# A Mamba-2 mixer in an fp32 decoder trunk: another order of its first projections, other owners of its buffers

## The chip, the cores and the metric

The kernel runs on one core of a Trainium2 chip. The metric is device time in microseconds for one launch, the median of three runs. The engines: PE (TensorE, matmuls), DVE (VectorE), ACT (ScalarE), POOL (GpSimd) and SP (SyncE, which here only issues DMAs). Lnnn is a line of the kernel before; behind the first changed line the kernel after has other numbers, by up to 16.

## What is computed

A decoder trunk of two layers on 256 tokens with D = 2048, in float32: an attention mixer (MLA), an MLP, a Mamba-2 mixer (SSM), an MLP, each with RMSNorm ahead and a residual around it. The change lies in the Mamba-2 mixer:

```python
def ssm_mixer(h, w_in, conv_w, conv_b, dt_bias, a_log, d_skip, norm_g, w_out):
    zxbcdt = h @ w_in                                   # 2048 x (4096 z + 4096 x + 1024 B + 1024 C + 64 dt)
    z, xbc, dt = jnp.split(zxbcdt, ...)
    xbc = silu(causal_depthwise_conv(xbc, conv_w, conv_b))      # width 4
    xs, b_in, c_in = jnp.split(xbc, ...)                        # 8 groups of 8 heads of 64
    dt = softplus(dt + dt_bias);  a = -exp(a_log)
    y = ssd_chunked_scan(xs, dt, a, b_in, c_in)                 # one chunk of 256 tokens here
    y = (y + d_skip * xs) * silu(z)
    y = group_rms_norm(y) * norm_g
    return y @ w_out
# the scan of one chunk, per group g and head h
    cum = cumsum(dt * a);  decay = exp(cum_l - cum_s) for s <= l
    y = ((c @ b.T) * decay) @ (x * dt)
```

## The kernel before

**Weights.** The products run in fp32r pieces: a weight tile of 128 x 1024 (a *unit*) comes in by DMA (`wraw`, six buffers), ACT rounds it to `wh` (L102), DVE forms the rest `wl = wraw - wh` (L103), and PE multiplies high and low parts (L339, L340, L343). A plain unit is 12 matmuls of 128x128 by 128x512. Units are taken in one fixed sequence through the whole kernel, and wraw520, wh520 and wl520 are those of unit 520. `wh` and `wl` have four buffers each, so ACT and DVE run up to four units ahead of PE.

**Seven-product pairs.** The first four x blocks of the input projection are done as two pairs, each by a scheme with seven products (M1, N7, N5, N6, N4, M2, N3) of four units where eight would stand. Such a unit is 6 matmuls (L1158 to L1160) and is used with sums of tokens (`sN5` and so on) and sums of weights, which DVE forms (L183) beside its own wl: 40 DVE operations for 28 units. N7's result holds one of the two `sm` banks of PSUM for the whole pair. Between the products stand plain units of other x blocks, the fillers; `woven` interleaves them by a model of PE's and DVE's time.

**Order.** PE's order is written by hand: the program text is its order. Small work is put among the units by `later(n, fn)`: fn runs n ticks on, and a tick is two plain units. The other engines' order comes from a scheduler that goes by dependencies and priorities; `behind(...)` ties an instruction behind the latest weight load or half.

**The mixer.** B and C come in two blocks each; `conv` transposes a block half into a PSUM bank (L1216), and the convolution along the free axis is one ACT operation (L1222) and three DVE operations (L1225) per 128 channels, out of that bank. The narrow dt block ends in a fold into an sm bank (L367) and a chain of small DVE and ACT operations. The x blocks are written to DRAM (`xD`) and read back shifted: `x_conv(g)` loads the group's tile `xtm`, its shifted copies `tap` and the taps' weights `cw` on SP's queue, DVE combines them (L1353, L1354). Per group `cb_group` forms c·bᵀ in an sm bank; `pump`, once each tick, takes a head's row of `cum` from DRAM, broadcast to 128 partitions (`cm`, issued on ACT's queue, L1407), and `head` turns it into the decay `mt` on ACT (L1417, L1419). `products` multiplies a group's heads (L1437) into both `yp` banks of PSUM, POOL adds the skip (L1441, with the gain `dsk`) and the far part (L1443). `z_block` gates; `words` has POOL copy parts of the result by DMA (`tr`, L308), PE transposes it into an sm bank (L322), ACT and DVE split it (L299, L300), and the so units multiply it. Gains (`dsk`, `sng`, 256 KB each) are loaded on SP's queue into two `gb` buffers (L391). `SSM_ORDER` is the order of the blocks: v is an x convolution (v1+2: two ticks late), z a gate block, o an output block.

## Time and profile before

| | before |
|---|---|
| median of three runs (lowest to highest) | 2331.21 us (2329.78 to 2332.99) |
| the profiled execution: its time; its span | 2331.0 us; 2329.2 us |
| PE, DVE, ACT, POOL busy, of the span | 2281.0, 1971.9, 1437.2, 254.7 us |
| mean granted clock of PE | 0.992 |
| DMA | 569.74 MB, mean 245 GB/s |

The span is the profiled execution from its first to its last instruction; 1.8 us of its time lie around it, and its time is 0.2 us under the median. A busy time is a sum over one engine; a matmul that waits on the pipeline counts as busy. In a row of the timeline stand the start, the length, the engine, the line, the output and inputs and, in brackets, how long the engine had been idle and what ended that. A window's row has the share of full speed that PE's clock was granted.

### The profile page before, as it was taken

Reading aid. Unit: us, or ns where it says so; the run is one execution under the profiler, and the core shown is the slowest. Engines: PE = TensorE matmul, PEld = TensorE weight load, DVE = VectorE, ACT = ScalarE, POOL = GpSimd, SP = SyncE. Lnnn points to the kernel's source line nnn. Section 1 sums busy time; section 2 is a strip of 40 time slices with the busy share of each in tenths; the row PEclk is TensorE's granted clock in tenths of the full one; section 3 lists DMA queues with packets and bytes.
Section 4 is the critical chain, followed back from the end, with each engine's and each line's share of the span. In section 5 each row is a group of like instructions: output and inputs, shape, how many; then the busy total and the mean of one; then the engine's idle time right before and its main releaser. Section 6 shows DMA issues by size and latency. Waiting matters only on the chain.

```text
span 2329.2 us, 30832 instructions
## 1 busy us (share of the span) xinstructions
PE 2281.0 (98%) x10881; PEld 1886.9 (81%) x10881; DVE 1971.9 (85%) x2257; ACT 1437.2 (62%) x2036; POOL 254.7 (11%) x323
## 2 busy tenths in 40 slices
PE   9999999999999999989998899999999999999999
PEld 7888888888888888877876677788888888888887
DVE  7786798899899888898768888876989899989985
ACT  7775566666666656556656665564666666666663
POOL 1540000000000000000001322230000000000000
PEclk9999999999999999999999999999999999999999
DMA  8545688888888877768886887777688888888875
GB/s 316 166 160 163 210 244 254 262 254 262 277 246 261 279 211 251 245 176 268 290 310 220 297 269 252 265 222 216 214 257 244 267 266 252 261 269 243 267 233 164
DMA packets 177050, 569.74 MB, mean 245 GB/s; under 512 B 20192, under 2 KB 29344, under 8 KB 176896
## 3 DMA queue, kind: packets, MB, share of 16 engines
q1 hardware_dynamic: 150112, 502.44, 64.6%
q0 software_dynamic: 15040, 52.68, 11.0%
q10 hardware_dynamic: 11744, 12.66, 1.8%
q8 instruction: 85, 1.39, 0.2%
q14 instruction: 69, 0.57, 0.1%
HBM read 542.23 MB, written 6.41 MB: 236 GB/s over the span
## 4 chain that ended last, share of the span: by engine, by line
PE 88%; DVE 5%; DMA 4%; ACT 2%; issue 1%; POOL 0%; SPq 0%; ACTq 0%; DVEq 0%
PE yp L619 9%; PE yp L618 9%; PE yp L617 9%; PE acc L339 8%; PE acc L343 8%; PE acc L340 8%; PE st L618 7%; PE st L619 7%; PE st L617 7%; DMA cm<-cumD 2%; DVE wl L103 2%; PE st L1160 1%; PE st L1158 1%; PE st L1159 1%; PE yp L339 1%
## 5 line engine op out<-in xcount | busy, mean ns | idle before, releaser
L102 ACT ACTIVATE wh<-wraw 128x1024 fp32r<-128x1024 f32 (+1 forms) x818 | 856.1, 1052 | 522.4 <-PE acc L340 183.9
L103 DVE TENSOR_TENSOR wl<-wraw,wh 128x1024 fp32r<-128x1024 f32 (+1 forms) x818 | 999.3, 1240 | 197.9 <-ACT wh L102 186.4
L617 PE MATMUL yp<-wh,k 128*128 128x512 f32 x896 | 349.3, 390 | 0.0
L619 PE MATMUL yp<-wh,k 128*128 128x512 f32 x896 | 348.8, 389 | 0.0
L618 PE MATMUL yp<-wl,k 128*128 128x512 f32 x896 | 348.6, 389 | 0.0
L102 ACT ACTIVATE wh<-wrx 128x1024 fp32r<-128x1024 f32 x192 | 203.3, 1059 | 169.8 <-PE yp L619 102.9
L103 DVE TENSOR_TENSOR wl<-wrx,wh 128x1024 fp32r<-128x1024 f32 x192 | 233.7, 1222 | 40.7 <-ACT wh L102 40.2
L339 PE MATMUL acc<-wh,k 128*128 128x512 f32 x496 | 197.6, 398 | 3.0 <-ACT wh L102 3.0
L619 PEld LDWEIGHTS yp<-wh,k 128*128 128x128 f32 x896 | 168.2, 188 | 35.1
L618 PEld LDWEIGHTS yp<-wl,k 128*128 128x128 f32 x896 | 168.2, 188 | 34.9
L617 PEld LDWEIGHTS yp<-wh,k 128*128 128x128 f32 x896 | 168.2, 188 | 34.8
L339 PE MATMUL acc<-wh,xt 128*128 128x512 f32 x480 | 193.0, 402 | 2.7 <-ACT wh L102 1.7
L340 PE MATMUL acc<-wh,k 128*128 128x512 f32 x496 | 193.8, 391 | 0.0
L340 PE MATMUL acc<-wh,xt 128*128 128x512 f32 x480 | 188.9, 394 | 0.0
L617 PE MATMUL st<-wh,xt 128*128 128x512 f32 x448 | 177.7, 397 | 0.0
L619 PE MATMUL st<-wh,xt 128*128 128x512 f32 x448 | 174.9, 390 | 0.0
L618 PE MATMUL st<-wl,xt 128*128 128x512 f32 x448 | 174.7, 390 | 0.0
L343 PE MATMUL acc<-wl,k 128*128 128x512 f32 x496 | 133.8, 392 | 4.5 <-DVE wl L103 4.5
L617 PE MATMUL st<-wh,sN 128*128 128x512 f32 x336 | 133.1, 396 | 0.0
L618 PE MATMUL st<-wl,sN 128*128 128x512 f32 x336 | 131.5, 391 | 0.9 <-DVE wl L103 0.8
L619 PE MATMUL st<-wh,sN 128*128 128x512 f32 x336 | 131.1, 390 | 0.0
L343 PE MATMUL acc<-wl,xt 128*128 128x512 f32 x480 | 129.4, 392 | 0.1
(343 smaller groups left out, 3700.2 us busy)
## 6 DMA issues: line engine op xcount, KB each, us to landing
wraw<-mi SPq DMA_DIRECT2D x256, 512.0 KB, 5.6
wraw<-mo SPq DMA_DIRECT2D x256, 512.0 KB, 5.4
wraw<-si SPq DMA_DIRECT2D x160, 512.0 KB, 5.3
wraw<-so SPq DMA_DIRECT2D x64, 512.0 KB, 4.7
wrx<-mi SPq DMA_DIRECT2D x56, 512.0 KB, 5.1
wrx<-mi POOLq DMA_DIRECT2D x56, 512.0 KB, 7.7
wraw<-wo SPq DMA_DIRECT2D x32, 512.0 KB, 3.9
tap<-xD SPq DMA_DIRECT2D x24, 512.0 KB, 7.4
```

The source lines that it names most:

```text
L102: self.last = nc.scalar.activation(h[:, v], raw[:, v], AF.Copy)
L103: self.last_lo = nc.vector.tensor_tensor(lo[:, v], raw[:, v], h[:, v].bitcast(F32), ALU.subtract)
L339: nc.tensor.matmul(accs[t][:, :n], ah, wh[:, q, :], start=first and kt + q == 0, stop=False)
L340: nc.tensor.matmul(accs[t][:, :n], al, wh[:, q, :], start=False, stop=False)
L343: nc.tensor.matmul(accs[t][:, :n], lhs(kt + q, t)[0], wl[:, q, :], start=False, stop=en and q == nk - 1)
L617: nc.tensor.matmul(b, ah, wh, start=first and q == 0, stop=False)
L618: nc.tensor.matmul(b, ah, wl, start=False, stop=False)
L619: nc.tensor.matmul(b, al, wh, start=False, stop=last and q == 1)
L1158: nc.tensor.matmul(bank[onto], ah, wh, start=done + q == 0 and not skip, stop=False, skip_group_check=skip)
L1159: nc.tensor.matmul(bank[onto], al, wh, start=False, stop=False, skip_group_check=skip)
L1160: nc.tensor.matmul(bank[onto], ah, wl, start=False, stop=done == 3 and q == 1, skip_group_check=skip)
```

## The change

It does seven things, all in the mixer; PE has the same matmuls in another order.

1. Order of the first blocks: B0, dt, C0 and x4 come as plain blocks before the pairs (B0, C0, dt before). The sums of tokens are made in ticks 5, 8 and 11 (0, 1 and 2 before). The fold of dt comes 2 ticks after its block (6 before).
2. Fillers: both pairs have 12 plain units (8 and 16 before): x5 and half of x6, then the rest of x6 and x7.
3. Shared buffers: the pools `xn` (sums N7 and N6, then `xtm`) and `rx` (weights of the pairs, then `tap`) live on through the mixer, so that the first convolution, `x_conv(0, 0)`, is called inside the second pair, once N5 and N6 are complete.
4. A convolution half of B and C is copied out of its PSUM bank by ACT (`held`), and always uses an sm bank (`wide=False`).
5. `pump` keeps four `cm` in flight and takes a head when more than two are there.
6. The gains of the groups are loaded on POOL's queue.
7. `SSM_ORDER`, the steps inside `x_conv` and the depth of `cb` (2 buffers in place of 5) follow.

On PE the first place is the fold of dt. Before, it stands in the first pair, behind C0's second half; `sm_755` is the half's bank, `sm_758` the fold's, `st` a product's sum, and 455 and 456 are units:

```order
L1216 MATMUL sm_755_9552<-ident_97,s2_741_9227 128x128
L1216 MATMUL sm_755_9552<-ident_97,s2_742_9229 128x128
L367 MATMUL sm_758_9569<-cst_96,s2_744_9270 128x64 x2
L1158 MATMUL st_750_9369<-wh456_9509,sN6_724_8955 128x512
L1159 MATMUL st_750_9369<-wh456_9509,sN6_725_8956 128x512
L1160 MATMUL st_750_9369<-wl456_9510,sN6_724_8955 128x512
```

After, it stands between two plain units, those of C0 (`acc`), ahead of the pairs:

```order
L343 MATMUL acc_722_9058<-wl433_9063,xt_677_8587 128x512
L343 MATMUL acc_723_9059<-wl433_9063,xt_677_8587 128x512
L367 MATMUL sm_733_9165<-cst_96,s2_721_9056 128x64 x2
L339 MATMUL acc_722_9058<-wh434_9080,xt_690_8693 128x512
L340 MATMUL acc_722_9058<-wh434_9080,xt_691_8694 128x512
```

No convolution half stands around it any more, and no product holds a bank.

On ACT the second place is a group's heads. Before (group 1), the loads of heads 12 and 13 and their use:

```order
L1407 DMA cm12_11368<-cumD_8833 128x256
L1407 DMA cm13_11370<-cumD_8833 128x256
L102 ACTIVATE wh549_11316<-wraw549_11173 128x1024
L1222 ACTIVATE s2_814_11285<-sm_813_11280,cst_96 128x256
L1417 ACTIVATE mt12_11437<-cm12_11368,pcum_8830 128x128 x2
L1419 ACTIVATE mt12_11437<-mt12_11437,lndt_8832 128x128 x2
L1417 ACTIVATE mt12_11437<-cm13_11370,pcum_8830 128x128
L102 ACTIVATE wh550_11334<-wraw550_11244 128x1024
```

After, the loads in that place are those of heads 14 and 15, and heads 12 and 13, which are used there, were loaded earlier:

```order
L1417 DMA cm14_11437<-cumD_8833 128x256
L102 ACTIVATE wh551_11374<-wraw551_11261 128x1024
L1232 ACTIVATE s2_821_11297<-s2_819_11286 128x512
L1417 DMA cm15_11439<-cumD_8833 128x256
L1427 ACTIVATE mt12_11515<-cm12_11368,pcum_8830 128x128 x2
L1429 ACTIVATE mt12_11515<-mt12_11515,lndt_8832 128x128
L102 ACTIVATE wh552_11392<-wraw552_11314 128x1024
```

Between load and use stood one unit's wh; now heads 14 and 15 are loaded before head 12 is taken.

On SP the third place is the first convolution's loads. Before, they stand at plain units, behind wraw525 and wraw527:

```order
L85 DMA wraw525_10552<-si 128x1024
L1348 DMA xtm0_10531<-xD_8834 128x2x512
L1336 DMA cw0_3_10571<-cwx 128x512
L1340 DMA tap0_2_10573<-xD_8834 128x2x512
L1336 DMA cw0_2_10575<-cwx 128x512
L1340 DMA tap0_1_10577<-xD_8834 128x2x512
L85 DMA wraw526_10579<-si 128x1024
L85 DMA wraw527_10597<-si 128x1024
L1336 DMA cw0_1_10615<-cwx 128x512
L1340 DMA tap0_0_10617<-xD_8834 128x2x512
```

After, they stand behind wraw520 and wraw522, which are products of the second pair:

```order
L85 DMA wraw520_10519<-si 128x1024
L1353 DMA xtm0_10539<-xD_8834 128x2x512
L1340 DMA cw0_3_10541<-cwx 128x512
L1344 DMA tap0_2_10543<-xD_8834 128x2x512
L1340 DMA cw0_2_10545<-cwx 128x512
L1344 DMA tap0_1_10547<-xD_8834 128x2x512
L85 DMA wraw521_10549<-si 128x1024
L85 DMA wraw522_10573<-si 128x1024
L1340 DMA cw0_1_10595<-cwx 128x512
L1344 DMA tap0_0_10597<-xD_8834 128x2x512
```

The loads moved forward by five units; xtm0 and tap0 now lie in the shared pools. In DVE's order after, the product `tap0_1` with `cw0_1` stands ahead of wl520.

Besides: group 7's two transposes stood ahead of unit 648 on PE and now stand ahead of unit 658, which reads them; in POOL's order each gain load stands directly behind the instruction that reads its buffer last, or that instruction's transposed words.

The diff, without the lines that only follow from these:

```diff
-    def gain_tile(self, src):
+    def gain_tile(self, src, queue=None):
         t = self.gb.tile([P, 512], F32, tag="gb", name=self.name("gb"))
-        self.nc.sync.dma_start(t, src)
+        (queue or self.nc.sync).dma_start(t, src)
...
         def put(name, src):
-            S[name] = [pool.tile([P, 8, P], F32R, name=self.name("s" + name)) for _ in range(2)]
+            if name in ("N7", "N6"):
+                S[name] = [xn.tile([P, 8, P], F32R, tag="xn", name=self.name("s" + name)) for _ in range(2)]
+            else:
+                S[name] = [pool.tile([P, 8, P], F32R, name=self.name("s" + name)) for _ in range(2)]
             self.split_out(*[v.rearrange("p k n -> p (k n)") for v in S[name]], src)
...
             if done == 3:
                 after(name)
+                if name in ("N5", "N6") and count.get("N5") == count.get("N6") == 4 and free:
+                    free()
             self.spend(1.36)
...
-                a = self.scratch()
+                a, held = self.scratch(), self.scratch()
+                nc.scalar.activation(held, b, AF.Copy)
...
-                    s, o = b[:, k * 256:(k + 1) * 256], a[:, k * 256:(k + 1) * 256]
+                    s, o = held[:, k * 256:(k + 1) * 256], a[:, k * 256:(k + 1) * 256]
...
-        def bc_block(name, i, lag=1, gap=2, wide=True):
+        def bc_block(name, i, lag=1, gap=2, wide=False):
...
         def dt_block():
-            self.narrow_block(("si", "dt", 0, 0), self.xT, dt_chain, 6)
+            self.narrow_block(("si", "dt", 0, 0), self.xT, dt_chain, 2)
...
-            pairs = [sp1.tile([P, S], F32, tag="dts", name=f"dt{i}", bufs=3).rearrange("p (i t h) -> p i t h", i=2, t=2) for i in range(3)]
+            pairs = [sp.tile([P, 512], F32, tag="cw", name=f"dt{i}", bufs=3)[:, :S].rearrange("p (i t h) -> p i t h", i=2, t=2)
+                     for i in range(3)]
...
-            self.later(4, cums)
+            self.later(3, cums)
...
-            t = sp2.tile([P, 384], F32, tag="cb", name=f"cb{g}", bufs=5)
+            t = sp2[0].tile([P, 384], F32, tag="cb", name=f"cb{g}", bufs=2)
...
         def x_conv(g, wait):
-            xt = sp2.tile([P, 2, 512], F32, tag="xtm", name=f"xtm{g}", bufs=4)
-            x = [xt[:, t] for t in range(2)]
-            cw, tap = {}, {}
+            cw, tap, xts = {}, {}, []
 
             def weight(k):
-                cw[k] = sp2.tile([P, 512], F32, tag="cw", name=f"cw{g}_{k}", bufs=3)
+                cw[k] = sp.tile([P, 512], F32, tag="cw", name=f"cw{g}_{k}", bufs=3)
                 nc.sync.dma_start(cw[k], d["cwx"][g][:, k * 512:(k + 1) * 512])
 
             def load(k):
-                tap[k] = sp2.tile([P, 2, 512], F32, tag="tap", name=f"tap{g}_{k}", bufs=3)
+                tap[k] = self.flow.pools["rx"].tile([P, 2, 512], F32, tag="rx", name=f"tap{g}_{k}")
                 nc.sync.dma_start(tap[k], x_rows(g, 0, 2, k))
...
             def whole():
-                nc.sync.dma_start(xt, x_rows(g, 0, 2))
+                xts.append(xn.tile([P, 2, 512], F32, tag="xn", name=f"xtm{g}"))
+                nc.sync.dma_start(xts[0], x_rows(g, 0, 2))
...
             def total():
-                tapped(0)
-                nc.vector.tensor_tensor(xt, xt, both(4), ALU.add)
-                tap[3] = sp2.tile([P, 2, 512], F32, tag="tap", name=f"th{g}", bufs=3)
+                with behind("last_lo"):
+                    plus(both(4))
+                    tapped(0)
+
+            def tanh():
+                tap[3] = self.flow.pools["rx"].tile([P, 2, 512], F32, tag="rx", name=f"th{g}")
                 with behind("last"):
-                    nc.scalar.activation(tap[3], xt, AF.Tanh, scale=0.5)
+                    nc.scalar.activation(tap[3], xts[0], AF.Tanh, scale=0.5)
 
             def silu():
-                nc.vector.scalar_tensor_tensor(xt, tap[3], 1.0, xt, ALU.add, ALU.mult)
+                with behind("last_lo"):
+                    nc.vector.scalar_tensor_tensor(xts[0], tap[3], 1.0, xts[0], ALU.add, ALU.mult)
 
             def ahead():
-                xg[g] = x
-                for i in range(8):
-                    hq.append((g, i))
+                x = xg[g] = [xts[0][:, t] for t in range(2)]
...
             self.later(wait, lambda: fetch(whole, lambda: weight(3), lambda: load(2), lambda: weight(2), lambda: load(1)))
             self.later(wait + 1, lambda: fetch(lambda: weight(1), lambda: load(0)))
-            self.later(wait + 2, lambda: cb_group(g))
             self.later(wait + 3, mult)
             self.later(wait + 4, lambda: tapped(1))
-            self.later(wait + 5, total)
-            self.later(wait + 6, lambda: (silu(), ahead()))
+            self.later(wait + 4, lambda: cb_group(g))
+            self.later(wait + 5, lambda: (total(), hq.extend((g, i) for i in range(8))))
+            self.later(wait + 6, tanh)
+            self.later(wait + 7, lambda: (silu(), ahead()))
 
         def pump():
             for _ in range(2):
-                if cms:
+                if len(cms) > 2 or cms and not hq:
                     g, i, cm = cms.pop(0)
                     head(g, i, cm)
                     if i == 7:
                         break
-            while hq and len(cms) < 2:
-                g, i = hq.pop(0)
-                cm = sp2.tile([P, S], F32, tag="cm", name=f"cm{8 * g + i}", bufs=4)
-                nc.scalar.dma_start(cm, cumD[8 * g + i:8 * g + i + 1].to_broadcast([P, S]))
-                cms.append((g, i, cm))
+            for _ in range(2):
+                if hq and len(cms) < 4:
+                    g, i = hq.pop(0)
+                    cm = sp2[0].tile([P, S], F32, tag="cm", name=f"cm{8 * g + i}", bufs=4)
+                    nc.scalar.dma_start(cm, cumD[8 * g + i:8 * g + i + 1].to_broadcast([P, S]))
+                    cms.append((g, i, cm))
...
-            dg = self.gain_tile(d["dsk"][g])
+            dg = self.gain_tile(d["dsk"][g], nc.gpsimd)
...
-                ng = self.gain_tile(d["sng"][g])
+                ng = self.gain_tile(d["sng"][g], nc.gpsimd)
...
+        xn = later.enter_context(self.tc.tile_pool(name="xn", bufs=4, reuse_waits="tile"))
+        self.flow.pools["rx"] = later.enter_context(self.tc.tile_pool(name="rx", bufs=4, reuse_waits="tile"))
         with ExitStack() as first:
             sp1 = first.enter_context(self.tc.tile_pool(name="ssm1", bufs=1, reuse_waits="tile"))
-            self.flow.pools["rx"] = first.enter_context(self.tc.tile_pool(name="rx", bufs=4, reuse_waits="tile"))
-            sums, steps = self.sums_of_tokens(sp1)
-            for n, fn in enumerate(steps):
+            sums, steps = self.sums_of_tokens(sp1, xn)
+            for n, fn in zip(SUMS_AT, steps):
                 self.later(n, fn)
             bc_block("B", 0)
-            bc_block("C", 0, 3, 3, False)
             dt_block()
+            bc_block("C", 0)
+            x_block(4)
             for p in range(2):
-                self.ssm_seven(sums, p, filler, lambda p, j, t, src, dst: put_x(2 * p + j, t, src, dst))
-        sp2 = later.enter_context(self.tc.tile_pool(name="ssm2", bufs=1, reuse_waits="tile"))
+                self.ssm_seven(sums, p, filler, lambda p, j, t, src, dst: put_x(2 * p + j, t, src, dst),
+                               (lambda: x_conv(0, 0)) if p else None)
+        sp2.append(later.enter_context(self.tc.tile_pool(name="ssm2", bufs=1, reuse_waits="tile")))
...
-SSM_FILLERS = [[("x", 4)], [("x", 5), ("x", 6)]]
-SSM_ORDER = ["v0", "x7", "v1+2", "B1", "C1", "v2", "z0", "v3+2", "z1", "z2", "v4", "z3", "v5+4", "o0a", "o0b", "v6+2", "z4",
-             "o1a", "v7", "o1b", "z5", "z6", "z7", "o2a", "o2b", "o3"]
+SUMS_AT = (5, 8, 11)
...
+SSM_ORDER = ["v1+3", "B1", "C1", "v2+1", "z0", "z1", "v3", "z2", "z3", "v4", "o0a", "o0b", "v5", "z4", "z5", "v6", "o1a", "v7+1",
...
     si("B", 0)
+    add(("si", "dt", 0, 0), d["sidt"], 16, 64)
     si("C", 0)
-    add(("si", "dt", 0, 0), d["sidt"], 16, 64)
+    si("x", 4)
```

More of the change, by code (lines that the diff above doesn't have):

```diff
@@ L1075, in whole @@
         def whole(i, t):
[L1076 to L1077 removed]
+            v = self.flow.pools["rx"].tile([P, 1024], F32, tag="rx", name=self.name("xf"))
             f[i, t] = v
@@ L1104, in sums_of_tokens, with ssm_seven @@
         return S, (one, two, three)
-    def ssm_seven(self, S, p, filler, out):
+    def ssm_seven(self, S, p, filler, out, free=None):
         nc = self.nc
@@ L1347, in whole @@
             def whole():
-                nc.sync.dma_start(xt, x_rows(g, 0, 2))
+                xts.append(xn.tile([P, 2, 512], F32, tag="xn", name=f"xtm{g}"))
+                nc.sync.dma_start(xts[0], x_rows(g, 0, 2))
             both = lambda k: cw[k].unsqueeze(1).to_broadcast([P, 2, 512])
+            plus = lambda v: nc.vector.tensor_tensor(xts[0], xts[0], v, ALU.add)
             def tapped(k):
                 nc.vector.tensor_tensor(tap[k], tap[k], both(k), ALU.mult)
-                nc.vector.tensor_tensor(xt, xt, tap[k], ALU.add)
+                plus(tap[k])
             def mult():
                 with behind("last_lo"):
-                    nc.vector.tensor_tensor(xt, xt, both(3), ALU.mult)
+                    nc.vector.tensor_tensor(xts[0], xts[0], both(3), ALU.mult)
                     tapped(2)
@@ L1545 @@
 TINY = 1.2e-38
-SSM_FILLERS = [[("x", 4)], [("x", 5), ("x", 6)]]
-SSM_ORDER = ["v0", "x7", "v1+2", "B1", "C1", "v2", "z0", "v3+2", "z1", "z2", "v4", "z3", "v5+4", "o0a", "o0b", "v6+2", "z4",
-             "o1a", "v7", "o1b", "z5", "z6", "z7", "o2a", "o2b", "o3"]
+SUMS_AT = (5, 8, 11)
+SSM_FILLERS = [[("x", 5, o) for o in range(8)] + [("x", 6, o) for o in range(4)],
+               [("x", 6, o) for o in range(4, 8)] + [("x", 7, o) for o in range(8)]]
+SSM_ORDER = ["v1+3", "B1", "C1", "v2+1", "z0", "z1", "v3", "z2", "z3", "v4", "o0a", "o0b", "v5", "z4", "z5", "v6", "o1a", "v7+1",
+             "o1b", "z6", "z7", "o2a", "o2b", "o3"]
 def woven(p):
@@ L1556, in woven @@
     second = [("M2", d) for d in range(4)] + [("N3", d) for d in range(4)]
-    units = [b + (o,) for b in SSM_FILLERS[p] for o in range(8)]
+    units = list(SSM_FILLERS[p])
     pe = 28 * 1.36 + 2.72 * len(units)
```

10 lines of the change are left out of this document (4 added, 6 removed).

## The prediction

> **What bounds the kernel now.** I read the busy times by stage first, then what TensorE (PE) waited for, then the granted clock, then DVE and ACT around each stall. The first view gives PE's busy time in the mixer (956 to 1580 us), before it and after it:
> ```profile
> 956.00:1580.00 624.00, 583.14 (x3004) 0.97 0.79 257
> 0.00:956.00 956.00, 952.75 (x4486) 1.00 0.76 239
> 1580.00:2329.20 749.20, 745.15 (x3394) 1.00 0.79 242
> ```
> The columns are window, length, PE busy (instructions), clock, DMA share and GB/s. PE is idle for 624.00 − 583.14 = 40.86 us in the mixer and for 3 to 4 us in each other part, and only the mixer has a clock below 1. So the kernel is bound by PE, and what can be won without removing PE work lies in the mixer. What PE waited for there:
> ```profile
> PE y L1437 <- DVE s L1225: 10.0, 1, 10.0
> PE sm L322 <- DVE k L300: 9.5, 1, 9.5
> PE sm L367 <- DVE s L1225: 8.1, 1, 8.1
> PE acc L339 <- ACT wh L102: 4.7, 4, 1.7
> PE acc L343 <- DVE wl L103: 4.5, 3, 2.9
> PE sm L1301 <- DVE k L300: 3.0, 1, 3.0
> ```
> (total us, times, longest). Four single stalls make 30.6 of the 40.9; late weight halves (wh, wl) make 9.2; the rest is 1.1. Each long stall is followed by a slow clock. These are the 5 us after the stalls that ended at 1038.79, 1241.50, 1303.75, 1346.45 and 1459.34:
> ```profile
> 1038.80:1043.80 5.00, 5.00 (x15) 0.56 0.00 0
> 1241.50:1246.50 5.00, 5.00 (x68) 0.69 0.74 287
> 1303.70:1308.70 5.00, 4.95 (x15) 0.50 0.75 254
> 1346.40:1351.40 5.00, 4.95 (x16) 0.66 0.80 257
> 1459.30:1464.30 5.00, 4.96 (x15) 0.66 0.74 215
> ```
> The work lost there is 5 × (0.44 + 0.31 + 0.50 + 0.34 + 0.34) = 9.65 us. Idle and clock together: 50.5 us. The change leaves PE's instructions what they were, so the floor is 2331.0 − 50.5 = 2280.5 us. Everything turns on how many of these stalls go and which come instead.
>
> **The stall at 1038.79, in the first pair.** PE waits for a PSUM bank. The rows, DVE (start, us) and PE:
> ```profile
> 1028.42 1.22 DVE L103 TENSOR_TENSOR wl<-wraw,wh 128x1024 fp32r<-128x1024 f32 x1
> 1029.56 1.22 DVE L103 TENSOR_TENSOR wl<-wrx,wh 128x1024 fp32r<-128x1024 f32 x1
> 1037.12 1.52 DVE L1225 SCALAR_TENSOR_TENSOR s<-sm,cst,s 128x255 f32<-128x255 f32 x3 [0.63 <-ACT s L1222]
> 1028.70 0.39 PE L1158 MATMUL st<-wh,sN 128*128 128x512 f32 x1
> 1030.07 0.60 PE L1216 MATMUL sm<-ident,s 128*128 128x128 f32 x4
> 1038.79 1.09 PE L367 MATMUL sm<-cst,s 128*128 128x64 f32 x4 [8.12 <-DVE s L1225]
> 1000.00:1030.00 30.00, 30.00 (x136) 24.81 (x135) 29.21 (x34) 20.16 (x23) 2.73 (x3) 1.00 0.79 217
> ```
> There are two sm banks. N7 of the pair holds one throughout; C0's second convolution half fills the other at 1030.07 and gives it back when DVE's six L1225 end at 1038.64, since they read PSUM and stand between weight operations. dt's fold (L367) is next in PE's order. DVE is full: 29.21 of 30 us (the last row's busy columns are PE, PE's loads, DVE, ACT, POOL). DVE's rows follow each other every 1.14 us and six matmuls of a product take 1.37 us (1028.70 to 1030.07), so a filler takes 2.74. The first pair has 28 products and 8 fillers: PE 28 × 1.37 + 8 × 2.74 = 60.3 us. DVE has 40 + 8 weight operations × 1.14 = 54.7, two C0 halves of six L1225 (1.52 / 3 = 0.51 each, 3.0 a half) add 6, and the bank sums and dt's chain of small operations some 5 (my estimate): about 66, more than PE has. After the change the pair has 12 fillers (PE 71.2) and DVE 52 × 1.14 = 59.3 plus some 3 for the bank sums; B0, dt and C0 come before it, under plain units in which PE takes 2.74 for each 1.14 of DVE. In the order the fold stands behind unit 433, ahead of the pairs. The stall goes, with its clock: −8.1 and −2.2.
>
> **The stall at 1241.50, at y0.** PE needs both yp banks for a group's products, and C1's half (wide=True) sits in one:
> ```profile
> 1234.54 0.48 DVE L1225 SCALAR_TENSOR_TENSOR s<-yp,cst,s 128x255 f32<-128x255 f32 x1
> 1239.85 1.50 DVE L1225 SCALAR_TENSOR_TENSOR s<-yp,cst,s 128x255 f32<-128x255 f32 x3
> 1241.50 0.80 PE L1437 MATMUL y<-xtm,mt 128*64 128x64 f32 x10 [9.96 <-DVE s L1225]
> ```
> After, the halves use sm only, and an ACT copy (`held`) empties the bank before DVE starts. Nearest row for that copy, 128x512 out of PSUM, is L299 below, 0.53 each. Eight copies are 4.3 us of ACT, which is at 20.16 of 30 us in the busiest stretch above; hidden, and where that cover fails each holds up one wh by 0.5. Six of DVE's operations then read SBUF; I take their 0.48 as unchanged. −10.0 and −1.6.
>
> **The stalls at 1303.75 and 1346.45.** Transposes and cb wait for an sm bank that DVE empties late. POOL's work on group 0 stretches two weight operations of DVE, and DVE is full for 34 us:
> ```profile
> 1285.18 6.03 DVE L103 TENSOR_TENSOR wl<-wraw,wh 128x1024 fp32r<-128x1024 f32 x2
> 1285.33 2.54 POOL L1441 TENSOR_TENSOR xtm<-xtm,gb 128x512 f32<-128x512 f32 x2
> 1303.02 0.68 DVE L300 TENSOR_TENSOR k<-sm,k 128x512 fp32r<-128x512 f32 x1
> 1270.00:1304.00 34.00, 33.38 (x35) 0.93 0.76 259
> ```
> What DVE does for a group is the same in both kernels. In the order, y0 to y7 stand behind weight units 543, 555, 567, 579, 591, 607, 619, 631 before, and behind 543, 557, 569, 583, 599, 615, 633, 641 after: where six of the seven periods had 12 units (32.9 us of PE), five now have 14 to 18, one 12, and the last 8. Two more units bring 5.5 us of PE and 2.3 of DVE, so DVE gains 3.2 us by them; the last period loses 6.4, of what the one before it (18) gained. I also ran DVE's order against PE's with these durations, and marked how far DVE's work ahead of a unit's wl outruns PE's. Before, that climbs by 7.6, 6.6 and 4.4 us exactly ahead of the three longest stalls; after, by never more than 2.6. I take both stalls as gone, −12.0 and −4.7 with their clock; the 2.6 comes back below.
>
> **The late weight halves.** ACT issues a head's `cm` load and reads it one tick (two units, 5.5 us) later:
> ```profile
> ACT mt L1417 <- DMA cm<-cumD: 28.0, 14, 4.9
> cm<-cumD ACTq DMA_DIRECT2D x64, 128.0 KB, 5.3
> 1430.21 0.69 ACT L1417 ACTIVATE mt<-cm,pcum 128x128 f32<-128x128 f32 x2 [3.84 <-DMA cm<-cumD]
> 1432.64 1.06 ACT L299 ACTIVATE k<-sm 128x512 fp32r<-128x512 f32 x2
> 1432.49 0.50 PE L339 MATMUL acc<-wh,k 128*128 128x512 f32 x1 [1.66 <-ACT wh L102]
> ```
> The load lands after 5.3 us in the median, so there is no margin; 14 of the heads made ACT wait, the wh behind them in ACT's order came late, and wl after it. The new pump keeps four loads in flight, and a head waits two ticks (11 us) for its load. In the order only the first two and the last two heads (0, 1, 60, 61) still stand one unit behind their load. −9.2, with −1.7 of clock at 1459.
>
> So far all 50.5 us are taken, the last 1.1 among them. **What comes instead:**
>
> *The first convolution in the second pair's tail.* It is now issued when N5 and N6 of the second pair are complete, and SP places its loads from wraw520 on, where units take 1.37 us each: four of 512 KB and three of 256 KB, 2.9 MB. Nothing before shows a convolution there; the nearest rows:
> ```profile
> DVE tap L1353 <- DMA cw<-cwx: 13.4, 5, 4.1
> tap<-xD SPq DMA_DIRECT2D x24, 512.0 KB, 7.4
> 1150.00:1180.00 30.00, 29.96 (x134) 24.52 (x133) 13.50 (x15) 16.20 (x32) 0.00 (x0) 1.00 0.92 341
> 1180.00:1210.00 30.00, 28.32 (x125) 22.59 (x123) 24.64 (x25) 19.72 (x33) 1.95 (x1) 1.00 0.92 325
> ```
> These are the windows in which the first two convolutions load today: 92% busy and 341 GB/s, and PE lost almost nothing beside it. At the full 341 GB/s the 2.9 MB are 8.5 us. DVE's tap0_1 product stands ahead of wl520, while its cw0_1 is issued behind wraw522; such a wait cost DVE up to 4.1 us. Lower end 0 (six raw buffers and the windows' 29.96 of 30), upper 8.5 + 2 of clock = 10.5; I take 4, nearer the rows of today's loads, since the units are now half as long.
>
> *Group 7's transposes.* Before, they stand ahead of unit 648 and are first read at 658; now they stand directly ahead of 658. PE waits for L299 (0.53) and two L300 (0.68 each) behind a wl or two: 1.2 to 4, taken 2.
>
> *The four heads that still stand at one unit.* ACT's waits were 28.0 / 14 = 2.0 each, and all of them together cost PE 9.2: 0 to 4, taken 2.
>
> *What is left of DVE's lateness* (2.6 at most, at a few places where cb and two transposes follow each other in two sm banks; `held`): 0 to 12 (the two transposing stalls back), taken 3. *Clock after all these*: 0 to 5 (three ramps like those above), taken 2.
>
> *The gain loads* (dsk, sng) go from SP's queue to POOL's: 16 issues.
> ```profile
> gb<-dsk SPq DMA_DIRECT2D x8, 256.0 KB, 4.2
> SPq L391 <- POOL xtm L1441: 12.4, 3, 7.1
> ```
> On SP they made the weight loads behind them wait for a buffer; six raw buffers hid that, and I count no gain. In POOL's order each now stands right behind the instruction that frees its buffer, and its reader comes a group later: 0.
>
> Sum: 2331.0 − 50.5 + 4 + 2 + 2 + 3 + 2 = 2293.5. The median of the runs stands 0.2 above the profiled run: 2294.
>
> [...] The clock was 0.66 after stalls of 3.0 and 2.9 us. [...]
> With `held`, L1225 reads two SBUF tensors where one was PSUM; POOL is busy for 1.95 of 30 us in the second of the windows above, so I charge nothing. [...]
>
> **The rivals.** *A, the first convolution collides.* The loads at the pair's tail push the weight loads back by their whole 8.5 us, DVE's wait for cw0_1 holds wl520 for 4.1 on top, and the clock falls: 8.5 + 4.1 + 3 in place of 4 gives 2305. For it: DMA at 0.92 there. Against it: SP issues wraw520 ahead of them. *B, DVE's lateness moves instead of going.* DVE's total is the same, and it is busy for 33 of 34 us around a group; if the transposes still meet an occupied sm bank in two groups (12.0 + 4.7) and the rest comes as taken, 2294 + 17 = 2311. For it: POOL's stretching of DVE remains. Against it: the longer periods. If that happens in four groups, +34 and no change: 2328. *C, slower: the gain loads in POOL's queue.* If POOL stood still for each load's buffer and landing, its own products, the transposed words and so the yT of each group would be late by 4.2 us, 16 times: 67 us, and 2294 + 67 = 2361. It decides from 37 / 16 = 2.3 us each on. For it: SP did wait up to 7.1 us for such a buffer. Against it: an issue doesn't wait for its landing, the order puts each behind its release, and the transposes come three ticks (16 us) after the words.
>
> **How the numbers follow.** The likeliest case has 0.62 and its own range is 2285 (new terms 4) to 2304; A has 0.15, B 0.12, its version with no change 0.04, C 0.07. A run tells about 0.2% from no change, 4.7 us: below 2326.5 is faster. So faster 0.89, same 0.04, slower 0.07. The range takes in the likeliest, A and most of B: 2284 to 2313; outside it lie C, the unchanged case and some of B.
>
> **What would show it.** In the profile after, PE's waits have no L367, y or sm line above 3 us; PE's busy time in the mixer is over 97% of it; the clock is 1.00 in nearly every slice; ACT's wait for `cm` falls from 28 us to under 8; PE's idle time between units 516 and 530 tells the first convolution's price. I am wrong if a new wait of over 8 us stands at the second pair's tail or at an early y, or if sm waits for k L300 remain.

## The result, and the profile after

| | before | after |
|---|---|---|
| median (lowest to highest) | 2332.08 us (2329.78 to 2332.99, 4 runs) | 2300.61 us (2297.53 to 2305.47, 4 runs) |
| the profiled execution: its time; its span | 2331.0; 2329.2 | 2302.0; 2300.2 |
| mean granted clock | 0.992 | 0.997 |

The ratio is 0.9868, 95% interval 0.9849 to 0.9888: faster by 31.5 us between the medians (1.3%). Forecast was 2294 with 2284 to 2313. PE's busy time by stage in the profile after (columns as before):

```profile
956.00:1580.00 624.00, 610.09 (x3150) 0.99 0.81 267
0.00:956.00 956.00, 952.94 (x4482) 1.00 0.76 238
1580.00:2300.20 720.20, 713.96 (x3253) 1.00 0.79 243
```

PE is idle for 13.9 us in the mixer (40.9 before) and for 9.3 elsewhere (7.3 before). What it waited for, total, times and longest:

```profile
PE st L1162 <- DVE wl L103: 8.1, 3, 5.3
PE sm L322 <- DVE k L300: 4.7, 2, 3.1
```

The lines of the fold (8.1), of y (10.0), of cb (3.0) and of the late wh (4.7) are gone. Idle time fell by 25.0 us in all, and PE's busy time by 4.0 (2281.0 to 2277.0), not by the 9.65 that the slow clock had cost: so 5.6 us of slow clock remain, after two new stalls. The three largest stalls left, and the 5 us behind each:

```profile
1096.12 0.79 PE L1162 MATMUL st<-wl,sN 128*128 128x512 f32 x1 [2.63 <-DVE wl L103]
1168.81 0.80 PE L1162 MATMUL st<-wl,xt 128*128 128x512 f32 x1 [5.34 <-DVE wl L103]
1407.58 0.45 PE L322 MATMUL sm<-ident,tr 128*128 128x128 f32 x3 [3.14 <-DVE k L300]
1096.10:1101.10 5.00, 4.98 (x12) 0.50 0.73 229
1168.80:1173.80 5.00, 4.99 (x12) 0.50 0.81 259
1407.50:1412.50 5.00, 4.92 (x78) 1.00 0.65 213
```

The second is the tail of the second pair. DVE there, and the stretch as a whole (DMA share 1.01, 358 GB/s):

```profile
1157.96 1.22 DVE L103 TENSOR_TENSOR wl<-wraw,wh 128x1024 fp32r<-128x1024 f32 x1
1166.39 1.22 DVE L1359 TENSOR_TENSOR tap<-tap,cw 128x1024 f32<-128x1024 f32 x1 [7.21 <-DMA cw<-cwx]
1167.54 3.49 DVE L103 TENSOR_TENSOR wl<-wraw,wh 128x1024 fp32r<-128x1024 f32 x3
1150.00:1172.00 22.00, 16.66 (x68) 0.89 1.01 358
```

DVE stands 7.2 us at the first tap's weights, and three wl whose inputs are there come right behind it. The first stall, at the change from the first pair to the second, is a weight load that arrives late:

```profile
1093.70 1.23 DVE L183 TENSOR_TENSOR wraw<-wraw,wraw 128x1024 f32<-128x1024 f32 x1 [3.17 <-DMA wraw<-si]
```

ACT's waits for `cm`, 28.0 us before:

```profile
ACT mt L1427 <- DMA cm<-cumD: 1.8, 4, 1.0
```

### The profile page after: what moved, and what is told of

It reads as the page before. It is cut to its first block, busy times and chain, and to the rows that moved or that the text cites. A ratio compares the mean times of both kernels' runs of the same rounds, so it can differ in the third digit from the quotient of the medians.

```text
span 2300.2 us, 30834 instructions
## 1 busy us (share of the span) xinstructions
PE 2277.0 (99%) x10881; PEld 1884.4 (82%) x10881; DVE 1961.4 (85%) x2257; ACT 1443.1 (63%) x2044; POOL 279.7 (12%) x339
## 4 chain that ended last, share of the span: by engine, by line
PE 89%; DVE 5%; DMA 3%; ACT 1%; issue 1%; POOL 0%; ACTq 0%; DVEq 0%; SPq 0%
PE acc L339 10%; PE acc L340 10%; PE acc L343 10%; PE yp L619 9%; PE yp L618 9%; PE yp L617 9%; PE st L618 7%; PE st L619 7%; PE st L617 7%; DVE wl L103 3%; DMA wraw<-mi 1%; PE st L1162 1%; PE yp L339 1%; PE yp L340 1%; PE yp L343 1%
## 5 line engine op out<-in xcount | busy, mean ns | idle before, releaser
L103 DVE TENSOR_TENSOR wl<-wraw,wh 128x1024 fp32r<-128x1024 f32 (+1 forms) x818 | 986.1, 1224 | 171.4 <-ACT wh L102 162.6
L199 POOL DMA_DIRECT2D wrx<-mi x56 | 49.0, 875 | 723.5 <-DVE wl L103 513.0
L343 PE MATMUL acc<-wl,k 128*128 128x512 f32 x496 | 132.7, 389 | 0.0
```

What stands on the lines that cost most here:

```text
L103: self.last_lo = nc.vector.tensor_tensor(lo[:, v], raw[:, v], h[:, v].bitcast(F32), ALU.subtract)
L199: nc.gpsimd.dma_start(st["b11"].tile, quarter(d, 1, 0), accum_op=ALU.add)
L343: nc.tensor.matmul(accs[t][:, :n], lhs(kt + q, t)[0], wl[:, q, :], start=False, stop=en and q == nk - 1)
```

## One part alone

My theory was that each part removes the stall I had put down to it, with its clock; the rival, that idle time moves. Four runs put one part (the last of them parts 1 and 2) into the kernel before; parts 3 and 7 were not run alone. Each comparison is against the kernel before in the same sitting (medians 2331.3 to 2332.2).

**The copy out of the bank (part 4).**

```diff
-                a = self.scratch()
+                a, held = self.scratch(), self.scratch()
+                nc.scalar.activation(held, b, AF.Copy)
...
-        def bc_block(name, i, lag=1, gap=2, wide=True):
+        def bc_block(name, i, lag=1, gap=2, wide=False):
```

> The kernel before with part 4 alone: ACT copies a convolution half out of its PSUM bank and the halves use sm banks only. My theory (a stall goes when the bank that PE waits for is given back earlier): the waits of 8.1 (fold of dt) and 10.0 us (y0) go, with their clock 2.2 and 1.6, so about 2331 - 22 = 2309; the two waits for k L300 stay. Rival (DVE's total is the same, so the idle time only moves): the fold goes through, and PE then meets weight halves (wl) that DVE delivers late; at most half is kept, 2320 or more, and PE's wait for wl L103 grows by 5 us or more.

Measured: 2323.62 us, ratio 0.997 (0.9952 to 0.9987). The waits at the fold (now 0.96 us) and at y are gone, and others have grown:

```profile
PE sm L322 <- DVE k L300: 11.9, 1, 11.9
PE acc L343 <- DVE wl L103: 7.5, 7, 2.9
PE sm L1384 <- issue: 3.1, 1, 3.1
```

k L300 was 9.5 and wl 4.5. Of the 21.9 us that I expected 7.7 stayed: the bank is free earlier, but DVE's work is not done earlier, and PE meets it at the next place. In the time the rival holds here; PE's wait for wl grew by 3.0 and not by the 5 that it asked for, and the rest went into the sm banks.

**The pump (part 5).**

```diff
-                if cms:
+                if len(cms) > 2 or cms and not hq:
...
-            while hq and len(cms) < 2:
+            for _ in range(2):
+                if hq and len(cms) < 4:
```

> The kernel before with the new pump alone (four cm loads in flight). My theory: the 28 us of ACT's waits for cm fall under 8, the late wh and wl (9.2 us of PE, 1.7 of clock) go, about 2320. Rival: heads come a tick later, DVE's product with cb with them, and the waits come back as waits of y or of k L300; 2328 to 2336.

Measured: 2306.01 us, ratio 0.9887 (0.9871 to 0.9904): 25.3 us where I expected 11, by far the most of any part. ACT's waits for `cm` fell to 3.9 us, and with them went not only the late halves:

```profile
PE sm L1383 <- DVE k L300: 8.9, 3, 5.1
PE sm L367 <- DVE s L1225: 8.2, 1, 8.2
PE y L1438 <- DVE s L1225: 3.4, 1, 3.4
```

The wait at the fold, which lies ahead of all heads, is as before. But y's is 3.4 in place of 10.0, the L300 waits are 8.9 in place of 12.5, and the late wh are gone.

**The place or the loads?** The new pump also takes the heads, and so y, one tick later. This run gives the kernel before that later place and leaves the loads one tick ahead of their use; PE's order is that of the run above.

```diff
-                for i in range(8):
-                    hq.append((g, i))
+                self.later(0, lambda: hq.extend((g, i) for i in range(8)))
```

> The kernel before with the old pump, but a group's heads taken one tick later: PE's order is then that of the run with the new pump (2306.0), while a cm load still stands one tick ahead of its use. If the new pump gains by the longer way of the loads, ACT's waits for cm stay near 28 us and the time near 2331 (2322 or more). If it gains by the place of the heads and of y, the time falls to 2306 (under 2314) with the waits for cm still there.

Measured: 2320.53 us, ratio 0.9954 (0.9937 to 0.9971), between the two.

```profile
ACT mt L1416 <- DMA cm<-cumD: 27.5, 12, 4.2
PE sm L1382 <- DVE k L300: 10.6, 3, 5.1
PE sm L367 <- DVE s L1225: 8.0, 1, 8.0
PE y L1436 <- DVE s L1225: 5.5, 1, 5.5
PE acc L343 <- DVE wl L103: 2.7, 2, 1.9
```

With the same waits for `cm` as before, the later place is worth 11.7 us (2332.2 to 2320.5), and the longer way of the loads the other 14.5 (2320.5 to 2306.0, in two sittings whose kernel before stood 0.9 apart). Neither theory alone held. The profiled executions are the fastest of the four runs here (2316.2) and the slowest with the pump (2309.0), so the rows can account for 7 of the 14.5 us only. They show one thing clearly: the late weight halves, 9.2 us before, are nearly gone here (2.7 in the last row), though ACT waits for `cm` as long as before.

**The gains on POOL's queue (part 6).**

```diff
-        self.nc.sync.dma_start(t, src)
+        (queue or self.nc.sync).dma_start(t, src)
...
-            dg = self.gain_tile(d["dsk"][g])
+            dg = self.gain_tile(d["dsk"][g], nc.gpsimd)
```

> The kernel before with the gains loaded on POOL's queue alone. My theory: nothing that can be measured, 2331 within 5. Rival C of the prediction: POOL stands still for the buffers, the transposed words come late, more than 2.3 us for each of 16 gains: 2368 or more. A third: SP's weight loads are no longer held up behind the gains, and some late wl go: 2322 to 2326.

Measured: 2332.62 us, ratio 1.0005 (0.9994 to 1.0015). Rival C is refuted, and so is a gain of more than 0.1%.

**The order of the first blocks (parts 1 and 2).**

```diff
             bc_block("B", 0)
-            bc_block("C", 0, 3, 3, False)
             dt_block()
+            bc_block("C", 0, wide=False)
+            x_block(4)
...
-SSM_FILLERS = [[("x", 4)], [("x", 5), ("x", 6)]]
+SSM_FILLERS = [[("x", 5, o) for o in range(8)] + [("x", 6, o) for o in range(4)],
+               [("x", 6, o) for o in range(4, 8)] + [("x", 7, o) for o in range(8)]]
```

> The kernel before with parts 1 and 2 alone (B0, dt, C0, x4 as plain blocks first, twelve fillers in each pair, z4 moved ahead so that the o blocks still find their groups gated). My theory: the 8.1 us at the fold go with 2.2 of clock, y0's wait and the late halves stay in kind; about 2321. Rival: the pairs' DVE work was not the reason, and another bank wait of 5 us or more stands in the first pair or at its neighbours: 2328 to 2336.

The run also makes the sums of tokens and the fold at their new ticks and takes z4 ahead of v5, which is no longer four ticks late.

Measured: 2323.04 us, ratio 0.9963 (0.995 to 0.9976), near the 2321 of my theory in size. The profiled execution is the slowest of the five (2326.5). The fold's wait is gone; y's is gone too, since the groups lie otherwise; but there are new ones:

```profile
PE acc L343 <- DVE wl L103: 7.6, 5, 3.0
PE sm L322 <- DVE k L300: 7.5, 1, 7.5
PE st L1160 <- DVE wl L103: 4.6, 2, 3.1
PE sm L1216 <- ACT s L1236: 4.6, 1, 4.6
1096.90 0.50 PE L1160 MATMUL st<-wl,sN 128*128 128x512 f32 x1 [3.06 <-DVE wl L103]
```

So the time is the one I gave, and not by the way I gave: the st wait in the last row is the one that the kernel after has at 1096.12.

## One part undone

The kernel after has its 2300.61 us from one sitting, and the runs from here on come from others; the median of the kernel before was 2332.1 us there, and 2332.0 or 2332.2 in these.

**The old pump in the kernel after.** The edit is that of the pump above, reversed.

> The kernel after with the old pump (two cm loads in flight, heads and y one tick earlier). If the pump is the largest part of the change also among the other parts: ACT's waits for cm are back at 20 us or more, late wh and wl with them, 2312 to 2322. If the other parts (longer periods between the groups, sm banks emptied by ACT) give the room that the pump gave in the kernel before, little is lost: 2300 to 2306.

Measured: 2313.83 us, ratio 0.9916 (0.9897 to 0.9934), 13.2 us more than the kernel after; ACT waits 22.1 us for `cm`, and PE's waits for wl of plain units (L343) are back at 6.4 us. The pump is worth half as much here as in the kernel before.

**Without the copy.** The edit of part 4, reversed, wide=True with it.

> The kernel after without the ACT copy of the convolution halves, which again use yp banks in turn. In the kernel before the copy alone gave 7.7 us. If that comes again, the waits of y0 or of an sm bank return: 2306 to 2312. If the new order keeps convolution halves away from y and from the fold: 2298 to 2303.

Measured: 2318.12 us, ratio 0.9936 (0.9917 to 0.9955), 17.5 us more.

```profile
1029.51 0.76 PE L339 MATMUL yp<-wh,xt 128*128 128x512 f32 x1 [6.56 <-DVE s L1229]
1242.97 3.47 PE L1446 MATMUL y<-xtm,mt 128*64 128x64 f32 x60 [4.71 <-DVE s L1229]
1422.16 0.53 PE L322 MATMUL sm<-ident,tr 128*128 128x128 f32 x3 [5.08 <-DVE k L300]
```

In the new order a half without the copy collides with a filler's yp bank (6.56) and with y (4.71). The copy alone gave 7.7 us, and taken away it costs 17.5: the new order needs it.

**The first convolution behind the pair.**

```diff
-                               (lambda: x_conv(0, 0)) if p else None)
+                               (lambda: x_conv(0, 3)) if p else None)
...
-SSM_ORDER = ["v1+3", "B1", "C1", "v2+1", "z0", "z1", "v3", "z2", "z3", "v4", "o0a", "o0b", "v5", "z4", "z5", "v6",
+SSM_ORDER = ["v1+6", "B1", "C1", "v2+3", "z0", "z1", "v3+1", "z2", "z3", "v4", "z4", "v5", "o0a", "o0b", "z5", "v6",
```

> The kernel after with the first convolution begun three ticks later, behind the second pair, as in the kernel before; the second and third follow by three and two ticks, z4 and v5 stand ahead of the first o blocks so that these find their groups gated. If beginning inside the pair is worth its price, the pair's tail loses its wait (8 us with its clock), and the groups come closer together later, with new waits of k L300 and wl of 8 us or more: 2300 or more. If it isn't, 2290 to 2296.

Measured: 2319.05 us, ratio 0.9934 (0.9911 to 0.9957), 18.4 us more. The wait at the second pair's tail is gone, and two later ones stand in its place:

```profile
1359.34 2.04 PE L1391 MATMUL sm<-s,cb 128*128 128x512 f32 x2 [8.82 <-DVE k L300]
1477.03 0.62 PE L322 MATMUL sm<-ident,tr 128*128 128x128 f32 x3 [8.96 <-DVE k L300]
```

y0 to y5 stand behind units 549, 565, 573, 585, 599, 607 here (543, 557, 569, 583, 599, 615 after), so four of the seven periods have 8 to 12 units, and two in the kernel after. That fits with beginning inside the pair as what buys the room between the groups. The run moves z4 and v5 as well, so the 18.4 are not the place of the first convolution alone.

## What is left in the kernel after

**DVE's order at the second pair's tail.** The first tap's product is tied behind the newest wl:

```diff
+            def once():
+                with behind("last_lo"):
+                    tapped(1)
...
-            self.later(wait + 4, lambda: tapped(1))
+            self.later(wait + 4, once)
```

> The kernel after, with the first tap's product and sum tied behind the newest wl in DVE's order, in all groups. If the 5.3 us at the second pair's tail come from DVE standing at cw0_1 with wl520 behind it, that wait goes with its slow clock: about 2300.6 - 8 = 2292. If the pair's tail is short of weights because 2.9 MB more are under way, PE's wait there stays at 3 us or more and the time at 2298 to 2303.

Measured: 2301.53 us, ratio 0.9871 (0.9856 to 0.9885): no gain. The stall went as the first theory says, yet the time stayed. The profiled execution is the slowest of the four (2305.6), and the stall at 1096 is 3.3 us in it:

```profile
1166.29 0.50 PE L1162 MATMUL st<-wl,sN 128*128 128x512 f32 x1 [0.53 <-DVE wl L103]
1405.10 0.63 PE L322 MATMUL sm<-ident,tr 128*128 128x128 f32 x3 [4.62 <-DVE k L300]
1457.71 0.62 PE L322 MATMUL sm<-ident,tr 128*128 128x128 f32 x3 [2.54 <-DVE k L300]
```

The tie holds for all groups, and where groups are dense, tap work that had been done early can stand ahead of L300: 3.14 and 1.58 became 4.62 and 2.54, with a slow clock behind both (0.72 from 1400 to 1412, 0.89 from 1448 to 1460). That this is the cause is argued from the edit; no run ties the first group alone.

**The loads' order there.**

```diff
-... fetch(whole, lambda: weight(3), lambda: load(2), lambda: weight(2), lambda: load(1)))
-            self.later(wait + 1, lambda: fetch(lambda: weight(1), lambda: load(0)))
+... fetch(whole, lambda: weight(3), lambda: load(2), lambda: weight(2), lambda: weight(1), lambda: load(1)))
+            self.later(wait + 1, lambda: fetch(lambda: load(0)))
```

> The kernel after, with each group's cw of tap 1 loaded ahead of that tap, so two weight loads and a tick earlier; DVE's order unchanged. By the order of the queue: cw0_1 lands some 3 to 6 us earlier, DVE's 7.2 us and PE's 5.3 us fall to 2 or less, 2293. By the transfers: DMA moves all it can there, cw0_1 lands hardly earlier and the weights behind it later; PE's wait stays at 3 us or more, 2298 to 2303.

Measured: 2296.74 us (2294.97 to 2298.43), ratio 0.9849 (0.9835 to 0.9864), 3.9 us under the kernel after and short of the 2293 that I gave; the slowest of its runs overlaps with the fastest of the kernel after (2297.5). DVE now waits for the tap itself, which lands after a median of 11.3 us in this stretch:

```profile
1159.98 1.23 DVE L1359 TENSOR_TENSOR tap<-tap,cw 128x1024 f32<-128x1024 f32 x1 [2.92 <-DMA tap<-xD]
1162.40 0.51 PE L1162 MATMUL st<-wl,xt 128*128 128x512 f32 x1 [1.04 <-DVE wl L103]
```

PE's 5.34 became 1.04, with three pieces of 0.2 to 0.4 behind it (2.0 in all). The order of the queue was most of the stall; the rest is the wait for the tap.

**Fillers for the pair's last products.**

```diff
-        if units and t >= rest and (op is None or work > t * ve / pe - 2):
+        keep = 2 if main else 0 if op is None or op is second and len(second) < 5 else 1
+        if len(units) > keep and t >= rest and (op is None or work > t * ve / pe - 2 or not main):
```

> The kernel after, with two of each pair's twelve fillers held back for its last products. If the 2.6 us at 1096 come from nine products in a row that ask for 512 KB every 1.37 us, they go with 3 of clock, and the wait at the second pair's tail falls too: 2292 to 2295. If they come from a single late transfer or differ from run to run, nothing changes: 2298 to 2303.

Measured: 2298.0 us (2294.68 to 2300.52), ratio 0.9854 (0.9839 to 0.9869). The stall at 1096 is gone in the profile, which is that of the fastest run (2294.7); the one at the second tail is 2.2 us in three pieces. The time lies at the edge of the range that I gave for no change. The medians are 2.6 us apart and the runs overlap (2297.5 to 2305.5 after), so the size is not settled.

**The three together.** These two edits, and cb of groups 5 and 6 a tick earlier:

```diff
-            self.later(wait + 4, lambda: cb_group(g))
+            self.later(wait + (3 if g in (5, 6) else 4), lambda: cb_group(g))
```

> The kernel after with cw of tap 1 loaded ahead of its tap, two fillers of each pair held back for its last products, and cb of groups 5 and 6 one tick earlier, away from the transposes that wait for the same two banks. If the three are separate waits they add: 2300.6 - 3.9 - 2.6 (as measured alone) - 4.7 (the two waits of k L300) and some of their clock, 2287 to 2291. If they share one cause (DVE late by a fixed amount of work), the waits move on to others: 2294 to 2298.

Measured: 2291.68 us (2290.95 to 2292.86), ratio 0.9822 (0.9804 to 0.984): 8.9 us under the kernel after and 40 under the one before, 0.7 above the range of the sum (2287 to 2291). The waits for k L300 fell from 4.7 to 0.9. What is left:

```profile
956.00:1580.00 624.00, 616.53 (x3197) 1.00 0.81 270
1157.85 1.23 DVE L1359 TENSOR_TENSOR tap<-tap,cw 128x1024 f32<-128x1024 f32 x1 [5.07 <-DMA tap<-xD]
1160.27 0.50 PE L1162 MATMUL st<-wl,xt 128*128 128x512 f32 x1 [3.71 <-DVE wl L103]
```

At the second pair's tail DVE waits 5.1 us for the tap, and PE 3.7 for that: the largest stall that remains. It looks like a matter of transfers now (386 GB/s from 1150 to 1172, a share of 1.04); no run moves the tap's own load.

## Why the prediction came out right, and where it was wrong

**The bound and the floor held.** PE's instructions are the same in number, nearly all of the gain is idle time of the mixer and its clock, and the time lies between the floor of 2280.5 and the kernel before. The profiled execution stands 21.5 us over the floor, where I had 13. The 21.5 are 13.9 of idle time in the mixer, 2.0 more of it elsewhere, and 5.6 of slow clock. Of the signs that I had named, ACT's waits for `cm` and PE's busy share (610.09 of 624 us, 97.8%) came as said; one sign of being wrong came too, since sm waits for k L300 remain (4.7 us, the longest 3.14).

**The terms that went.** All four long stalls and the late wh are gone in the kernel after, so the sum was right to take all 50.5 us. The step that failed is their division among the parts, *"the late weight halves: −9.2, with −1.7"* above all. Taken alone the pump gave 25.3 where that step gives 10.9, the copy 7.7 where its two stalls give 21.9 (the fold's too, as I wrote ahead of that run), the order 8.3 where the fold gives 10.3. The sum did not depend on this division only because all parts were made together.

The step had the path wrong in two ways. The place of the heads and of y counts by itself: one tick later, with the waits for `cm` unchanged, was worth 11.7 us and took most of the late halves away. And the longer way of the loads does more than the late halves. Ahead of y0 ACT had stood 12.6 us for `cm` (1164 to 1193), with the wh that DVE needs behind it. DVE's busy time from 1150 to 1240, in the kernel before, with the later place alone and with the pump:

```profile
1150.00:1240.00 90.00, 64.96 (x70) 0.97 0.87 310
1150.00:1240.00 90.00, 64.95 (x69) 1.00 0.89 307
1150.00:1240.00 90.00, 69.55 (x76) 0.98 0.93 335
```

With the pump DVE is 4.6 us of work further on, which fits with y's wait of 3.4 in place of 5.5 and 10.0. Ahead of the stall at 1303.75 ACT had waited for 3.1 us only; that DVE was then 33.38 of 34 us busy because it had to catch up is argued, not shown.

The parts also need each other: single gains of 25.3, 7.7, 8.3 and −1 (the gains on POOL, no difference) add up to 40 and the change gave 31.5, while without the copy or without the pump it gives 14 or 18.

**The four long stalls.** *The fold:* gone, as by the count of fillers; yet the copy alone removes it too (0.96 left), and in the new order without the copy a wait of 6.6 us stands near it. *y0:* gone by the copy, as said; the longer cm distance alone leaves 3.4. *k L300:* the longer periods and the run of DVE's order against PE's foretold that nearly all of it goes, with some left where cb and two transposes meet in two banks. That is where the 3.14 and 1.58 stand (ahead of units 599 and 615), 4.7 in place of 3; in the run with all three edits, which moves cb of two groups, 0.9 are left (4.3 and 4.8 with either of the others alone). For the two stalls before, the prediction wrote 12.0 us and 4.7 of clock; its rows give 12.5 (9.5 + 3.0) and 4.2, the same sum.

**The terms that came.** *The first convolution in the pair:* taken 4, measured 5.34 of PE and a clock of 0.50 behind it. The mechanism was the one named, DVE's product with cw0_1 ahead of wl520; its size was off since I took DVE's longest wait for cw (4.1) from a stretch at 341 GB/s, and it was 7.2 where these loads come on top of the pair's own. Of rival A the second half came, and 7.9 of its 15.6 us (5.34, and 2.6 of clock); that the weight loads came late by the whole 8.5 us is not seen, since three wl whose inputs were there stood behind DVE's wait, and tying that product behind wl took 5.34 to 0.53. *The change from the first pair to the second:* no term of mine; 2.63 and a clock of 0.50. With the bank wait of 8.1 us gone PE no longer leaves the loads that pause; that this is why it appeared is not shown, and the copy alone speaks against it, where the bank wait is gone as well and no st wait is over 0.7. With the new order of the blocks alone the stall is there (3.06), and holding back two fillers removed it in two profiles, so it comes with that order. *Group 7:* taken 2, measured 0.30 + 0.62, which stand behind 1580 and are 0.9 of the 2.0 elsewhere. *The heads:* taken 2, ACT waits 1.8 us for `cm` and PE shows none of it. *`held` beside POOL:* charged with nothing, and so measured; the median of the 48 convolution operations is 477 ns after (478 and 480 before), and one of them, beside POOL's far part, took 1098. *Clock:* taken 2, measured 5.6. This is the largest miss of the sum.

**The rivals.** B is seen in the copy alone and in the order alone, where waits moved on to L300 and wl; with all parts together it is not. C is refuted by the gains alone. The gain loads cost nothing and bring nothing, as taken.

## What to carry to other kernels

In this kernel a wait in ACT's order was priced by what stood behind it, not by the idle time that names it: 28 us of ACT's waits for small loads stood in PE's own waits as 9.2 us of late halves. A tick of delay took most of these away with the waits still there, for 11.7 us; the longer way of the loads, which took the waits away, gave another 14.5. Ask of each stall how the named engine came to be late, and follow that back before giving the stall to the buffer that it waits for. And try the parts of a large change one by one in both directions: here one part alone gives most, one is worth nothing, and the copy is worth more with the others than without.

## What the runs showed of the hardware

The slow clock does not follow from a stall's length alone. In the kernel after, a stall of 2.63 us was followed by 5 us at 0.50, one of 3.14 by 1.00; in the run with cw first 2.49 was followed by 1.00, and 2.64 at a later place by half speed. In the mixer the granted clock is 1.00 or 0.50 in the traces of the kernels before and after, and a value between is a mean of both. Before, the slow stretches begin at 1032.94, 1234.33, 1299.18, 1346.97 and 1459.61 and last 10.24, 10.24, 10.24, 3.41 and 3.41 us; after, they begin at 1095.49 and 1167.17 and last 6.82 us each. All these lengths, and the distances between the beginnings in one trace, are whole multiples of 3.41 us, a raster of steps; the clock in the windows of the other twelve traces fits such steps too. What tells the stalls above apart is how long PE was busy within a step. Each pair of rows is the step that holds most of one of these stalls and the step behind it, for 2.63 and 3.14 in the kernel after and then for 2.49 and 2.64 in the run with cw first:

```profile
1092.07:1095.49 3.42, 1.42 (x7) 1.00 0.94 379
1095.49:1098.90 3.41, 2.78 (x7) 0.50 0.53 171
1402.69:1406.10 3.41, 1.74 (x12) 1.00 0.24 67
1406.10:1409.51 3.41, 1.94 (x52) 1.00 0.78 278
1094.42:1097.83 3.41, 1.66 (x7) 1.00 0.55 191
1097.83:1101.24 3.41, 3.41 (x16) 1.00 0.79 262
1398.21:1401.62 3.41, 1.38 (x34) 1.00 0.78 288
1401.62:1405.03 3.41, 3.41 (x45) 0.50 0.56 165
```

In the kernels before and after the clock halved seven times in the mixer, each time at the end of a step in which PE was busy for 1.42 us or less; behind steps with 1.74 us or more it stayed. It came back at the end of a step with 3.07 us or more, and not behind one with 2.78. The shortest single stalls that the clock halved behind are two of 1.80 us, with the order alone and with the old pump in the kernel after (clock 0.86 from 1280 to 1292 and from 1304 to 1316, which is one step at 0.50):

```profile
1282.90 0.50 PE L339 MATMUL acc<-wh,xt 128*128 128x512 f32 x1 [1.80 <-ACT wh L102]
1304.72 1.51 PE L343 MATMUL acc<-wl,xt 128*128 128x512 f32 x4 [1.80 <-DVE wl L103]
```

They left PE 1.6 us of their step (3.41 − 1.80). So, as an estimate from these traces, a single stall of under 1.8 us keeps the clock, and one of up to twice that keeps or loses it by where it falls on the raster. In the kernel after the slow stretches last from 1095.49 to 1102.31 and from 1167.17 to 1173.99, and PE is back at 1096.12 and 1168.81: half of 6.2 + 5.2 is 5.7 us, against the 5.6 of the sum.

That a stall of about the same length is followed by 3 us or more at 0.50 in one place and by none in another may be part of why runs of the kernel after lie 8 us apart; this was not traced.

At the second pair's tail DMA moved 407 GB/s over 12 us in the run with all three edits, against 341 in the window of the prediction, and a 512 KB tap took 10.9 us in the median to land there and not 7.4.

```profile
1160.00:1172.00 12.00, 11.73 (x45) 0.86 1.03 407
```
